# More projection work in program order ahead of the triangular solve's first product

## The chip, the cores and the metric

The kernel runs on one core of a Trainium2 chip. The time is the device time of one execution in microseconds (us), as the median of several runs. Three runs of the kernel before gave 3366.3, 3369.54 and 3373.71 us. One further execution was recorded by the hardware profiler; all durations quoted below come from it.

The engines are called as in the profile: PE (TensorE matmul), PEld (its weight loads), DVE (VectorE), ACT (ScalarE), POOL (GpSimd) and SP (SyncE, whose queue issues nearly all DMAs here).

## The reference, cut to what matters

Two models run one after the other on 512 tokens of width 1024. The change touches only the mixer of the first model, which occurs twice (two layers). In each layer it computes, in outline:

```
proj = rmsnorm(x) @ w_in                      # q,k,v of attention; q,k,v of delta net; z; two gates
y_attn = grid_attention(rope(q), rope(k), v) @ w_o_attn
...
a_kk  = strictly lower part of (k_beta @ k.T) * decay      # 64 x 64, per head, chunk and direction
t_inv = triangular_solve(eye + a_kk, eye)                  # "the solve"
...
for chunk in chunks:                                       # "the scan"
    v_new = u - w @ state;  o = q_dec @ state + qk @ v_new
    state = state * g_tot + k_dec.T @ v_new
...
mixed = sigmoid(gate0) * y_attn + sigmoid(gate1) * (norm(o) * silu(z) @ w_o_dn)
x = x + mixed @ w_out
```

## The kernel before, in words

Activations lie with features on the 128 partitions and the 512 tokens along the free dimension. A weight matrix comes in 1 MB pieces of 256 columns (`fetch`, L465; two buffers), is split into a high and a low part by an ACT cast and a POOL subtraction (`wload`, L478 and the helper `tt`, L384; four buffers each), and multiplies the split activations in three matmuls per 128 x 128 block (`proj`, L491, L494, L495). One projection of 128 output columns over 1024 inputs is 24 matmuls of 512 columns; one over 512 inputs is 12. Results land in one of two PSUM banks (`psb`) until DVE or ACT has read them.

The mixer (`_mix`) is written as several Python generators that emit instructions piece by piece. Each `yield` gives a number, an estimate of how long that piece takes. `Side` (L1065) takes such a main generator and, after each of its pieces, lets side generators emit until their own sum has caught up. So the numbers decide only where in the program text a piece of side work stands. These generators matter here:

- `solve` (L1020) loads the 64 triangular matrices into the tile N with two DMAs (from `scrT`, L1023, and from `scrN`, L1024), yields, and then does 30 steps on DVE. Each step is one product into a PSUM bank and one addition back into N (both through L384) and yields 2.1 * (2j(31-j)+66)/960, together 26.0. A memset of the diagonal (L1035) follows in program order, then five copies, and the results go out by DMA (L1050). The PSUM bank is the only one of its kind in this stage (`psg`, one buffer by `banks(2, 3, 1)`, L1096); the attention core needs the same bank for its value products (L976).
- `qkv` (L894): projection of the attention key (6), then its norm, rotation (`turn`, L887), the value projection, eight copies (L912) and the splits of key and value (6).
- `queries(g)` (L916): two query projections (6 each), then norm, rotation and eight small DMAs (2).
- `gate_logits` (L1003): eight projections of the first gate (G1 to G8 below) and eight of the second (H1 to H8), 6 each.
- `core` (L941): the attention itself, with `queries(1)` in its middle; it is given with a factor 0.6.
- `scan` (L1243): sixteen steps of the delta net's scan, with a factor 0.25; beside it `branch` (L1012) emits eight output projections of 12 matmuls (B1 to B8), 3 each. While the scan runs, each gate or branch projection is pinned behind the last matmul of the scan step emitted before it.

The program order is not yet the order of the engine queues. The whole program is laid out by the tile framework (L1800, `schedule_with_timeline_sim=True`), which fills each engine's queue by its own forecast of when operands will be ready; program order sets only the priority among instructions that it takes to be ready. Semaphore waits, once placed, hold up everything behind them in the same queue.

The part that sets the order around the change is this (L1102 to L1114):

```python
heads = chain(qkv(), queries(0))
side = Side(merge(heads, islice(gates, G2)), gates)
side.beside(solve(at), R2)
...
side.gens.append(islice(gates15, 8 - E1 - E2))
side.beside(core(), R4)
last.append(pv_last[0])
for _ in islice(gates15, E2):
    pass
```

with G2 = 2, E1 = 1, E2 = 3, R2 = 1, R4 = 0.6.

Of the kernel before, what the change touches and what calls it, by code (L numbers as in the profile page):

```python
# [305 lines left out]
class Prog:  # L306
# [341 lines left out]
    def _mix(self, l, nm, nxt, mp):  # L648
# [371 lines left out]
        def solve(sp):  # L1020
            tmp, pt = sp.tile([P, 1024], F32, name="ntmp"), self.psg()
            Nm = N[:, :4096].rearrange("p (j i) -> p j i", j=64)
            nc.sync.dma_start(out=Nm[64:128], in_=scrT.rearrange("j c p (h i) -> (c p h) j i", h=2))  # L1023
            nc.sync.dma_start(out=Nm[0:64], in_=scrN.rearrange("c p (h j) i -> (c p h) j i", h=2))  # L1024
            yield 5

            Nh = N.rearrange("p (a x) -> p a x", a=2)[:, :, :2048].rearrange("p a (j i) -> p a j i", i=64)
            for j in range(1, 31):
                n = 31 - j
                t = pt[:, :2 * j * n].rearrange("p (a c i) -> p a c i", a=2, c=j)  # L1030
                self.tt(t, Nh[:, :, 0:j, j:j + 1].broadcast_to((P, 2, j, n)),
                        Nh[:, :, j:j + 1, j + 1:32].broadcast_to((P, 2, j, n)), ALU.mult)
                self.tt(Nh[:, :, 0:j, j + 1:32], Nh[:, :, 0:j, j + 1:32], t, ALU.add)
                yield 2.1 * (2 * j * n + 66) / 960.0
            nc.vector.memset(N[:, 0:4096:65], 1.0)  # L1035


            fw, bw = Nm[0:64], Nm[64:128]
            i0, i1 = slice(0, 32), slice(32, 64)
            flip = lambda v: v.rearrange("p j i -> p i j")  # L1040
            first = tmp[64:128].rearrange("p (j i) -> p j i", j=32)
            nc.gpsimd.tensor_copy(bw[:, i1, i0], bw[:, i1, i1])
            nc.scalar.copy(fw[:, i1, i0], flip(fw[:, i0, i0]))
            nc.vector.tensor_copy(first, flip(bw[:, i0, i0]))
            nc.vector.tensor_copy(bw[:, i1, i1], flip(bw[:, i1, i0]))
            nc.scalar.copy(bw[:, i0, i0], first)
            for s_ in range(4):
                for d in range(2):
                    c = 3 * d + (1 - 2 * d) * s_
                    nc.sync.dma_start(out=scrI[d][c].rearrange("c p h j i -> (c p h) (j i)"),  # L1050
                                      in_=N[d * 64 + c * 16:d * 64 + c * 16 + 16, :4096])
            yield 5
# [49 lines left out]
# [3 lines that stand above are left out]
        for _ in heads:  # L1105
            pass
# [698 lines left out]
```

## Time and profile before

| | |
|---|---|
| three runs | 3366.3, 3369.54, 3373.71 us |
| profiled execution, whole time | 3364.51 us |
| its span, first to last instruction | 3362.7 us |
| mean granted TensorE clock | 0.986 of full speed |
| PE busy | 3198.5 us, 95% of the span |
| DVE, POOL, ACT busy | 55%, 51%, 45% |

In a row of instructions the columns are: start in us, duration in us (of all in the row), engine, line, operation, output<-inputs, shapes and count; in brackets the idle time of the engine just before and what ended it. In a row of waits: engine, tile and line that waited, what it waited for, us in total, times, longest. In a table of stretches: the stretch, its length, then for each engine busy us and number of instructions, the granted TensorE clock, the DMA engines' busy share and GB/s. The first mixer's solve, attention and scan lie between 160 and 444 us of the span, the second's between 1016 and 1301 us.

### The profile page before, as it was taken

The page shows a single profiled execution, that of the slowest core. Times are in us where ns is not written, and L with a number is a line of the kernel's source. Part 1 is how long each engine was busy: PE and PEld are TensorE (multiplying, and loading weights), DVE is VectorE, ACT ScalarE, POOL GpSimd, SP SyncE. Part 2 cuts the span into 40 slices and gives each one's busy share as a digit, 9 for nine tenths or more (in the row PEclk, how much of TensorE's full clock was granted, in tenths as well). Part 3 has the DMA queues.
Part 4 walks back from the last instruction along what each step waited for, and adds up shares of the span by engine and source line. Part 5 has one row for each costly group of instructions (what it writes and reads, how often), then busy time and mean ns, then how long its engine had stood idle before and what let it go on. Part 6 is the DMA issues. An engine that isn't in the chain of part 4 may idle for free. (4 is left out here: it accounts for less than half of the span.)

```text
span 3362.7 us, 47054 instructions
## 1 busy us (share of the span) xinstructions
PE 3198.5 (95%) x17342; PEld 2643.8 (79%) x17342; DVE 1832.8 (55%) x3549; ACT 1499.9 (45%) x2804; POOL 1719.1 (51%) x1453
## 2 busy tenths in 40 slices
PE   8988799999998889999999998999999999999999
PEld 6767678888776677788887777878888888888887
DVE  7687556463678855555366675453223676453222
ACT  5646444343564643443353335543334455544332
POOL 4542375444554236544456556565556336555554
PEclk9999999999999999999999999999999999999999
DMA  4632532222355254322222113234223223222222
GB/s 155 179 94 67 136 118 99 97 92 94 125 162 136 69 124 129 126 90 99 100 102 88 63 47 129 91 124 132 90 99 110 73 69 126 95 91 93 99 100 88
DMA packets 142013, 353.03 MB, mean 105 GB/s; under 512 B 44079, under 2 KB 81327, under 8 KB 113112
## 3 DMA queue, kind: packets, MB, share of 16 engines
q1 hardware_dynamic: 140352, 346.53, 32.0%
q10 hardware_dynamic: 1432, 3.49, 0.4%
q8 instruction: 138, 2.26, 0.3%
q14 instruction: 91, 0.75, 0.1%
HBM read 316.34 MB, written 34.16 MB: 104 GB/s over the span
## 5 line engine op out<-in xcount | busy, mean ns | idle before, releaser
L384 POOL TENSOR_TENSOR wlo<-wraw,whi 128x512 fp32r<-128x512 f32 (+2 forms) x1044 | 1353.1, 1299 | 1420.8 <-ACT whi L478 1382.6
L478 ACT CAST whi<-wraw 128x512 fp32r<-128x512 f32 (+2 forms) x1044 | 633.4, 608 | 1141.0 <-PE psb L494 863.7
L491 PE MATMUL psb<-act,whi 128*128 128x512 f32 x1888 | 750.8, 398 | 25.4 <-ACT whi L478 12.6
L495 PE MATMUL psb<-act,wlo 128*128 128x512 f32 x1888 | 746.3, 396 | 0.6 <-POOL wlo L384 0.4
L494 PE MATMUL psb<-act,whi 128*128 128x512 f32 x1888 | 746.3, 395 | 0.6 <-DVE act L277 0.6
L491 PEld LDWEIGHTS psb<-act,whi 128*128 128x128 f32 x1888 | 359.0, 190 | 101.9 <-ACT whi L478 14.1
L495 PEld LDWEIGHTS psb<-act,wlo 128*128 128x128 f32 x1888 | 358.0, 190 | 76.5 <-POOL wlo L384 3.0
L494 PEld LDWEIGHTS psb<-act,whi 128*128 128x128 f32 x1888 | 358.6, 190 | 73.7 <-DVE act L277 2.0
L384 DVE TENSOR_TENSOR x<-psb,x 128x512 f32<-128x512 f32 x168 | 115.1, 689 | 380.3 <-PE psb L495 380.0
L491 PE MATMUL ps<-act,whi 128*128 128x512 f32 (+1 forms) x720 | 282.8, 393 | 3.4 <-ACT rB L303 3.4
L494 PE MATMUL ps<-act,whi 128*128 128x512 f32 (+1 forms) x720 | 282.2, 392 | 0.0
L495 PE MATMUL ps<-act,wlo 128*128 128x512 f32 (+1 forms) x720 | 281.9, 391 | 0.0
L491 PE MATMUL psb<-mid,whi 128*128 128x512 f32 x704 | 277.1, 394 | 1.0 <-DVE x L384 1.0
L495 PE MATMUL psb<-mid,wlo 128*128 128x512 f32 x704 | 276.3, 393 | 0.0
L494 PE MATMUL psb<-mid,whi 128*128 128x512 f32 x704 | 273.9, 389 | 0.0
L491 PEld LDWEIGHTS ps<-act,whi 128*128 128x128 f32 (+1 forms) x720 | 135.0, 188 | 34.3 <-ACT rB L303 4.9
L495 PEld LDWEIGHTS ps<-act,wlo 128*128 128x128 f32 (+1 forms) x720 | 135.0, 188 | 29.7
L494 PEld LDWEIGHTS ps<-act,whi 128*128 128x128 f32 (+1 forms) x720 | 135.0, 187 | 29.3
L495 PEld LDWEIGHTS psb<-mid,wlo 128*128 128x128 f32 x704 | 132.3, 188 | 30.5
L491 PEld LDWEIGHTS psb<-mid,whi 128*128 128x128 f32 x704 | 132.7, 188 | 29.2 <-DVE x L384 1.5
L494 PEld LDWEIGHTS psb<-mid,whi 128*128 128x128 f32 x704 | 132.2, 188 | 29.2
L384 DVE TENSOR_TENSOR cv<-ps,cv 128x512 f32<-128x512 f32 (+1 forms) x60 | 41.5, 692 | 188.7 <-PE ps L495 106.8
(431 smaller groups left out, 5441.9 us busy)
## 6 DMA issues: line engine op xcount, KB each, us to landing
wraw<-in_wup SPq DMA_DIRECT2D x44, 1024.0 KB, 4.8
wraw<-in_fup SPq DMA_DIRECT2D x44, 1024.0 KB, 4.8
wraw<-in_win SPq DMA_DIRECT2D x38, 1024.0 KB, 4.8
wraw<-in_wdn SPq DMA_DIRECT2D x16, 1024.0 KB, 4.8
wraw<-in_evin SPq DMA_DIRECT2D x16, 1024.0 KB, 4.8
wraw<-in_xakv SPq DMA_DIRECT2D x16, 1024.0 KB, 4.9
wraw<-in_fdn SPq DMA_DIRECT2D x16, 1024.0 KB, 4.9
wraw<-in_odin SPq DMA_DIRECT2D x12, 1024.0 KB, 4.8
```

The lines of the kernel that those rows point to most:

```text
L384: getattr(self.nc, eng).tensor_tensor(out, a, b, op)
L478: nc.scalar.copy(hi, part)
L491: mm = nc.tensor.matmul(ps, hi[:, i], acts[k][:, 0, :n], start=k == 0, stop=False)
L494: nc.tensor.matmul(ps, hi[:, i], acts[k][:, 1, :n], start=False, stop=False)
L495: nc.tensor.matmul(ps, lo[:, i], acts[k][:, 0, :n], start=False, stop=k == kc - 1)
```

## The change

One number changes: what `solve` yields between its two loads and its first product.

```diff
@@ -1022,7 +1022,7 @@
             Nm = N[:, :4096].rearrange("p (j i) -> p j i", j=64)
             nc.sync.dma_start(out=Nm[64:128], in_=scrT.rearrange("j c p (h i) -> (c p h) j i", h=2))
             nc.sync.dma_start(out=Nm[0:64], in_=scrN.rearrange("c p (h j) i -> (c p h) j i", h=2))
-            yield 5
+            yield 18
 
             Nh = N.rearrange("p (a x) -> p a x", a=2)[:, :, :2048].rearrange("p a (j i) -> p a j i", i=64)
             for j in range(1, 31):
```

The program order that follows from the numbers, with j1 to j30 for the solve's steps, q0 and q1 for the two groups of queries (a, b: projections; c: norm and rotation) and "core" for pieces of attention:

```
before: load qkvA j1-j3 G1 j4-j10 qkvB j11-j15 G2 j16-j21 q0a j22-j28 q0b j29 j30 end q0c
        | core with G3 G4 G5 G6 q1a G7 q1b q1c G8 H1 H2 H3 | H4 H5 H6
        | scan0 H7 ... scan6 B1 ... scan9 B2 ... scan12 B3 ... scan15 B4 | B5 B6 B7 B8 H8
after:  load qkvA G1 qkvB j1 G2 j2-j9 q0a j10-j15 q0b j16-j20 q0c j21 j22 G3 j23-j30 G4 end
        | core with G5 G6 G7 G8 q1a H1 q1b q1c H2 H3 H4 | H5 H6 H7
        | scan0 B1 ... scan3 B2 ... scan6 B3 ... scan9 B4 ... scan12 B5 ... scan15 B6 | B7 B8 H8
```

No instruction is added, removed or altered.

## Rows read from the trace of the kernel before

**Rows 1.** The page of the profile: span, busy time, and the group of POOL's weight subtractions.

```profile
span 3362.7 us, 47054 instructions
PE 3198.5 (95%) x17342; PEld 2643.8 (79%) x17342; DVE 1832.8 (55%) x3549; ACT 1499.9 (45%) x2804; POOL 1719.1 (51%) x1453
...
L384 POOL TENSOR_TENSOR wlo<-wraw,whi 128x512 fp32r<-128x512 f32 (+2 forms) x1044 | 1353.1, 1299 | 1420.8 <-ACT whi L478 1382.6
```

**Rows 2.** Stretches: busy us of each engine, clock; the first mixer, one later stretch.

```profile
192.40:208.50 16.10, 16.09 (x66) 13.26 (x67) 15.29 (x25) 5.79 (x10) 11.22 (x8) 0.86 0.27 83
208.50:244.70 36.20, 34.88 (x160) 27.16 (x158) 35.79 (x77) 18.53 (x39) 13.50 (x11) 1.00 0.27 95
244.70:248.40 3.70, 0.00 (x0) 0.00 (x0) 3.67 (x10) 0.00 (x0) 1.02 (x1) 0.96 0.00 0
248.40:269.30 20.90, 17.19 (x109) 14.71 (x110) 15.39 (x26) 17.90 (x35) 1.86 (x1) 0.93 0.51 102
295.70:325.70 30.00, 25.21 (x162) 20.21 (x161) 24.46 (x50) 23.55 (x54) 1.65 (x2) 1.00 0.12 40
422.30:443.60 21.30, 21.30 (x104) 17.47 (x101) 15.18 (x32) 7.29 (x13) 9.93 (x8) 1.00 0.21 63
650.00:700.00 50.00, 50.00 (x221) 41.25 (x221) 20.22 (x23) 16.81 (x27) 23.85 (x18) 1.00 0.27 96
```

**Rows 3.** Waits of PE, 150 to 215 us, then 1016 to 1067 us (second mixer).

```profile
PE ps L416 <- ACT cv L884: 6.3, 1, 6.3
...
PE ps L416 <- ACT cv L884: 6.0, 1, 6.0
```

**Rows 4.** The DVE queue in order of time around the first product, both mixers.

```profile
183.76 0.23 DVE L384 TENSOR_TENSOR ps<-N 128x60 f32<-128x60 f32 x1 [5.41 <-DMA N<-scrT]
...
184.06 0.11 DVE L1035 MEMSET N<- 128x64 f32 x1
...
184.47 0.69 DVE L384 TENSOR_TENSOR th<-th,cv 128x512 f32<-128x512 f32 x1
...
186.57 0.34 DVE L384 TENSOR_TENSOR ps<-N 128x168 f32<-128x168 f32 x1
...
1033.37 0.69 DVE L384 TENSOR_TENSOR th<-th,cv 128x512 f32<-128x512 f32 x1 [0.66 <-POOL th L384]
1040.15 0.23 DVE L384 TENSOR_TENSOR ps<-N 128x60 f32<-128x60 f32 x1 [6.09 <-DMA N<-scrT]
```

**Rows 5.** The ACT queue: readers of the query projections q0a and q1a, q1b.

```profile
191.75 0.60 ACT L884 ACTIVATE cv<-psb 128x512 f32<-128x512 f32 x1 [0.95 <-DVE ka L502]
...
267.11 0.70 ACT L883 ACTIVATE th<-psb,vect 128x512 f32<-128x512 f32 x1
...
269.15 0.71 ACT L883 ACTIVATE th<-psb,vect 128x512 f32<-128x512 f32 x1
```

**Rows 6.** Waits of PE, 215 to 300 us, then the scan, 345 to 422 us.

```profile
PE ps L976 <- DVE N L384: 3.8, 1, 3.8
...
PE ps L1202 <- DMA kes<-dnscr: 5.6, 2, 3.1
```

**Rows 7.** DVE groups by operation, 150 to 270 us: the solve's products and additions.

```profile
L384 DVE TENSOR_TENSOR ps<-N 128x60 f32<-128x60 f32 (+14 forms) x30 | 21.6, 719 | 5.7 <-DMA N<-scrT 5.4
L384 DVE TENSOR_TENSOR N<-N,ps 128x60 f32<-128x60 f32 (+14 forms) x30 | 14.9, 495 | 0.3
```

**Rows 8.** The tail behind the scan: DVE, then POOL, in order of time.

```profile
436.20 1.33 DVE L1016 SCALAR_TENSOR_TENSOR x<-x,psb 128x512 f32<-128x512 f32 x2
437.45 2.43 DVE L1294 SCALAR_TENSOR_TENSOR of<-ps,vect,z 128x256 f32<-128x256 f32 x6
...
440.22 2.56 POOL L502 TENSOR_TENSOR ydn<-of,ydn 128x512 fp32r<-128x512 f32 x2 [1.58 <-ACT ydn L500]
```

**Rows 9.** The DVE queue: readers of the gate projections G3 and G4.

```profile
200.69 0.69 DVE L384 TENSOR_TENSOR x<-psb,rB 128x512 f32<-128x512 f32 x1 [0.53 <-PE psb L495]
...
209.50 0.68 DVE L384 TENSOR_TENSOR x<-psb,rB 128x512 f32<-128x512 f32 x1
```

## The prediction

> **What bounds the kernel now.** I read the page first: PE is busy for 95% of 3362.7 us [rows 1], so only stretches in which PE stands idle, or work that PE does anyway but at another place, can move the time. Then I split the first mixer into stretches (the second repeats them) and compared each with a later stretch that PE fills without a gap [rows 2]. That stretch also gives the price of a projection: 221 matmuls in 50.0 us are 0.226 us each, so a gate projection (24) is 5.4 us and a branch projection (12) is 2.7 us. Third, the waits of PE: near the solve's start the longest is 6.3 us, in the second mixer 6.0 us [rows 3]; in both PE waits for the square of a query projection, L884 on ACT. Fourth, the queues behind that wait. ACT's L884 had to wait until DVE was done with the split of the rotated key, because it writes into a buffer that this split reads [rows 5]. And DVE had stood still for 5.4 us (6.1 in the second mixer) at the solve's first product, which waited for the load of N [rows 4]. So the load's lateness passes through the DVE queue and the ACT queue to PE.
>
> What matters most is what the DVE queue shows about order. The memset L1035 comes last of the solve's DVE work before the copies in program order, yet it runs behind the first product [rows 4]. The rotation's last addition (th<-th,cv) belongs to qkvB, which the program emits after j10, yet in the second mixer it runs ahead of j1, and in the first only j1 and the memset's neighbours pass it [rows 4]. So program order is priority only; an instruction is queued when the layout forecasts its operands ready, and the layout forecast the load to land some 5 us before it did.
>
> **The change part by part.** No instruction is new; everything is a matter of place. The profiled execution took 3364.5 us, of which the span is 3362.7; it lies 5.0 us under the median of 3369.5. The terms below are differences and are put on the median.
>
> (a) *The head.* G1 and qkvB now precede j1. G1 and G2 were done before the load landed, and qkvB's chain up to the value projection as well, so their new priority moves nothing. At the moment when the layout took N as landed, j1 was the one ready instruction on DVE: in the first mixer even the memset followed before the rotation's last addition [rows 4]. A lower priority does not hold back an instruction that has no competitor. I therefore expect j1 in its old place and the stall of 5.4 and 6.1 us to stay. What moves are the eight copies (L912) and the key's splits, which now pass the second addition and the third step; those three instructions cost some 0.2 to 0.35 us each (the third product: 0.34 [rows 4]). L884 comes forward by so much: 0.6 us taken, ends 0 and -0.9.
>
> (b) *The attention.* From the solve to the start of the scan the program now holds 15 gate projections, not 14: +5.4 us of PE work. What can hide it: PE idles for all of 244.7 to 248.4, when the core's value product waits for the solve's last addition (same bank, 3.8 us [rows 6]), for 20.9 - 17.2 = 3.7 us of 248.4 to 269.3, and for 4.8 us of 295.7 to 325.7 [rows 2]. In the first two PE has no projection at all, because both psb banks hold q1a and q1b, whose readers on ACT run only at 267.1 and 269.2 [rows 5]. After the change G7 and G8 go ahead of q1a, and H1 stands between q1a and q1b, so in those 25 us one bank stays free for H1 and then q1b: 10.8 us of work over 7.4 us of idle time. ACT, busy for 17.9 of 20.9 us there [rows 2], must cast their weights in between. I take 4.0 us as hidden: +1.4 us. Ends: nothing hidden +5.4; all 7.4 hidden -2.0.
>
> (c) *The scan.* The pinned work inside it has the same sum, 13.5 us (H7, B1 to B3 before; B1 to B5 after), but half of the 5.4 us at its start goes to step 3. PE waits for DMA-loaded keys (kes) twice there, 5.6 us in all [rows 6], the first time 2.5 us long, close behind step 3. B2 fits into it: -2.0 us taken. Ends -2.6 (the whole wait) and +2.7 (B2 lands ahead of a chain step that waited for nothing).
>
> (d) *The tail.* Behind the last scan step PE had five branches and H8, 21.3 us without a gap [rows 2]; now three branches and H8, 5.4 us less. But the first two operands of the next product (ydn) are written by POOL until 442.8 [rows 8], less than a us before the old end of that cover at 443.6. The chain that makes them gets faster only by the two branch readers (1.33 us) ahead of its scalings on DVE [rows 8]. So the tail ends at about 441.5 and PE idles for some 3 us: -2.1 us taken. Ends -0.8 (chain unmoved) and -5.4 (the cover was the limit).
>
> (e) *The solve's end.* j10 and later lose priority to q0a, q0b and q0c, j23 and later to G3. DVE is full there (35.8 of 36.2 us [rows 2]), but G3 and G4 were already done at 200.7 and 209.5 [rows 9], before the solve's middle, so the set of instructions ahead of the solve's last addition hardly changes: 0, with the ends in (b).
>
> Sum per mixer: -0.6 + 1.4 - 2.0 - 2.1 = -3.3 us; two mixers -6.6 us: 3369.5 - 6.6 = **3362.9 us**. A measurement of this kernel tells about 0.2%, 6.7 us, from no change, so this lies on the edge between faster and the same.
>
> The solve's products read both inputs from SBUF, its additions one from PSUM, and the products took 21.6 us against 14.9 us for the same elements [rows 7]; what else reads SBUF meanwhile may be the cause of these 6.7 us (R3). The Trainium skill ("SBUF — State Buffer", section "SBUF: two separate sides") has a rule that speaks against the change here: a DVE instruction with two SBUF inputs and a GpSimd instruction exclude each other for a whole instruction. By that rule the solve would get longer with every POOL subtraction put beside it; the products' excess agrees with it.
>
> **The rivals.**
>
> *R1: the change does what its place in the program says.* The products fall behind the key's tail, DVE copies and splits while the load is under way, L884 comes some 5 us earlier, and PE's wait of 6.3 and 6.0 us shrinks to about 1. PE's clock, 0.86 in the 16.1 us behind the wait [rows 2], where some matmuls run at the lower of its two levels, would gain up to 2.3 us. Price: about -6 us per mixer on top of the sum, 3362.9 - 12 = 3351 us. For it: in the second mixer j1 follows the rotation's addition directly, so a small shift of the forecast would let all copies pass. Against it: j1 stood alone when it was queued.
>
> *R2: slower, by lost cover.* The work that (b) puts ahead of the scan hides nothing, since PE's holes there are made by waits on DVE and ACT that move along with the projections, and the tail does not shorten because its own chain ends it. The place is the stretch from 244.7 to 325.7 and ydn behind the scan; the price is +5.4 - 0.8 = +4.6 us per mixer, 3369.5 + 9.2 = 3379 us. It decides if less than about 1 us of the 5.4 is hidden. For it: ACT's load in (b), and ydn's end at 442.8 [rows 8].
>
> *R3: the solve ends later.* Two more gates beside the solve bring four more POOL subtractions of 1.3 us [rows 1]; each in front of a product they would add up to 5.2 us per mixer to the wait of 3.8 us [rows 6], and with the other terms 3369.5 + 10.4 - 6.6 = 3373 us. Against it: G3 and G4 ran beside the solve before [rows 9].
>
> *R4: nothing.* The layout is greedy, so projections go where PE was free in either case, and all terms cancel: 3369 us.
>
> **How the numbers follow.** The sum as forecast, 0.55: it stands on the edge, so 0.27 faster, 0.25 the same, 0.03 slower. R1, 0.15, all faster. R2, 0.12, slower; R3, 0.03: 0.02 the same, 0.01 slower. R4, 0.15: 0.11 the same, the rest split. Together faster 0.44, the same 0.38, slower 0.18. The range goes from below R1 (two more us per mixer for the clock, 3347) to R2 less its last 2 us (3377); the likeliest case alone has 3356 ((d) at its lower end) to 3371 ((b) with nothing hidden).
>
> **What would show it.** Right: DVE still idles for 5 to 6 us on the load of N with j1 ahead of most copies; the wait of PE for L884 falls by less than 1 us; projection matmuls appear between 245 and 269 us; a branch fills the first wait for kes; a gap of 2 to 4 us opens on PE ahead of the first ydn product. Wrong: the eight copies ahead of j1 and PE's wait near 1 us (R1); no projections between 245 and 269 us and the scan starting 4 to 5 us later (R2); the value product's wait for N above 6 us (R3).

## The result and the profile after

The change makes the kernel slower. Four runs gave 3391.37 to 3400.86 us, median 3394.78, against 3369.5 us; the ratio is 1.0084, with an interval of 1.0063 to 1.0105, about 28 us (the two medians differ by 25.3). The profiled execution has a span of 3389.6 us, 26.9 more than before. The page, its lines as in [rows 1]:

```profile
span 3389.6 us, 47035 instructions
PE 3215.7 (95%) x17342; PEld 2653.6 (78%) x17342; DVE 1836.7 (54%) x3549; ACT 1500.2 (44%) x2804; POOL 1722.2 (51%) x1453
```

The same work on every engine, so the time went into waits and a lower clock, and the PE line tells how much into each. For the same 17342 matmuls PE is busy for 3215.7 us, not 3198.5: 17.2 of the 26.9 us. The granted clock, 0.981 instead of 0.986 over the span, comes to the same by an estimate: 3389.6 x 0.019 - 3362.7 x 0.014 = 17.3 us. Only the other 9.7 us are idle time of PE.

A residual addition behind the first mixer comes 16.9 us later than before, one behind the second 26.9 us later, and that stays to the end: the loss lies in the two mixers. I cut each mixer at five events that both traces show: the value projection read by PE (L524), the core's first value product (L976), the square sums of q1 (L416), the last value product, the last output product of the scan (L1236), the first product with ydn (L491). Lengths in us, first / second mixer:

| stretch | before | after |
|---|---|---|
| 1: head and solve | 70.0 / 72.7 | 70.8 / 70.0 |
| 2: first value product to q1's sums | 20.8 / 20.9 | 31.2 / 32.9 |
| 3: to the last value product | 56.6 / 56.7 | 58.1 / 58.1 |
| 4: gates and scan | 96.5 / 96.0 | 100.8 / 96.8 |
| 5: tail | 21.2 / 21.2 | 17.5 / 17.5 |

The ten stretches hold 21 of the 26.9 us, stretch 2 alone 10.4 and 12.0; the rest lies outside these cuts. Of the first mixer, the kernel after (columns as in [rows 2]; the cuts are rounded to 0.1 us):

```profile
180.00:250.80 70.80, 64.38 (x277) 51.07 (x278) 65.60 (x128) 30.44 (x58) 29.90 (x22) 0.93 0.30 88
250.80:282.00 31.20, 22.80 (x134) 18.66 (x133) 18.28 (x30) 19.20 (x40) 5.91 (x5) 0.95 0.43 102
282.00:340.10 58.10, 48.20 (x263) 38.87 (x262) 43.41 (x85) 34.25 (x73) 13.66 (x10) 0.94 0.11 32
340.10:440.90 100.80, 82.59 (x1349) 69.08 (x1348) 53.05 (x131) 41.66 (x100) 35.54 (x61) 0.92 0.58 127
440.90:458.30 17.40, 15.77 (x76) 12.89 (x76) 14.90 (x32) 6.71 (x12) 6.63 (x5) 1.00 0.24 67
```

And the kernel before, cut at the same events:

```profile
178.40:248.40 70.00, 58.70 (x252) 46.42 (x252) 63.14 (x129) 28.40 (x56) 27.58 (x21) 0.92 0.32 91
248.40:269.30 20.90, 17.19 (x109) 14.71 (x110) 15.39 (x26) 17.90 (x35) 1.86 (x1) 0.93 0.51 102
269.30:325.90 56.60, 51.37 (x287) 41.75 (x285) 44.46 (x86) 35.67 (x75) 16.26 (x12) 1.00 0.14 47
325.90:422.40 96.50, 78.13 (x1349) 66.02 (x1348) 52.67 (x130) 42.12 (x101) 35.58 (x61) 0.98 0.56 130
```

The counts of PE matmuls tell what moved, since a gate is 24: one gate more in stretch 1 (252 to 277) and in stretch 2 (109 to 134), one less in 3 (287 to 263), and two branches of 12 less in 5. Stretch 1 took its gate in 0.8 us, and stretch 3 gave nothing back for the one that it lost: it ran at a granted clock of 0.94, not 1.00. In stretch 2 PE is busy for 5.6 us more and idle for 4.7 us more. The waits of PE, 150 to 215 us, the second mixer's head, and 250 to 284 us, which answer to [rows 3, 6]:

```profile
PE ps L416 <- ACT cv L884: 4.0, 1, 4.0
...
PE ps L416 <- ACT cv L884: 2.4, 1, 2.4
...
PE psb L491 <- DVE gt L384: 5.1, 1, 5.1
```

The wait at the head shrank from 6.3 and 6.0 us; the one for `gt` is new. DVE's queue answers to [rows 4, 9] and names its cause:

```profile
184.10 0.23 DVE L384 TENSOR_TENSOR ps<-N 128x60 f32<-128x60 f32 x1 [4.19 <-DMA N<-scrT]
184.36 0.22 DVE L384 TENSOR_TENSOR N<-N,ps 128x60 f32<-128x60 f32 x1
184.39 0.11 DVE L1035 MEMSET N<- 128x64 f32 x1
184.62 0.29 DVE L384 TENSOR_TENSOR ps<-N 128x116 f32<-128x116 f32 x1
...
185.60 3.46 DVE L912 COPY cv<-th 32x512 f32<-32x512 f32 x8
...
264.47 0.69 DVE L384 TENSOR_TENSOR gt<-psb,rB 128x512 f32<-128x512 f32 x1 [5.76 <-DMA ti<-N]
...
1052.54 3.46 DVE L912 COPY cv<-th 32x512 f32<-32x512 f32 x8
...
1060.65 0.23 DVE L384 TENSOR_TENSOR ps<-N 128x60 f32<-128x60 f32 x1 [3.92 <-DMA N<-scrT]
```

`gt<-psb,rB` reads H1's PSUM bank. Its output tile `g1` (L1107) carries the tag "N": it takes the place of the solve's own tile, which is free only when the solve's eight transfers out (L1050) have landed. SyncE's queue shows these:

```profile
251.29 9.34 SPq L1050 DMA_DIRECT2D ti<-N  x8
```

So H1's projection is done, its bank stays taken until 264.5, q1a holds the other, and q1b's projection starts only at 265.22, after PE has idled for 5.07 us. Its matmuls start 0.43 us apart up to 267.94 and 0.23 us apart from 268.35 on: behind the wait PE ran at the lower of its two clock levels. ACT reads q1a and q1b 12.7 us later than in [rows 5]:

```profile
279.84 0.70 ACT L883 ACTIVATE th<-psb,vect 128x512 f32<-128x512 f32 x1
...
281.88 0.70 ACT L883 ACTIVATE th<-psb,vect 128x512 f32<-128x512 f32 x1
```

In the scan (waits of PE, 339.9 to 458.4 us) the wait for keys fell from 5.6 us [rows 6] to 3.2, as forecast, but a step of `join` (L1180, which puts the solve's results together for the scan) now waits behind a weight subtraction on POOL:

```profile
PE ps L1173 <- ACT offd L1165: 4.2, 4, 2.1
PE ps L1180 <- POOL wlo L384: 3.2, 1, 3.2
PE ps L1202 <- DMA kes<-dnscr: 3.2, 2, 2.8
```

The two cancel: in stretch 4 PE is idle for 18.2 us, 18.4 before. That it is 4.3 us longer is PE's busy time for the same 1349 matmuls, 82.59 us at a clock of 0.92 against 78.13 at 0.98.

In the tail, where [rows 8] show POOL's ydn, PE now waits for both halves of it:

```profile
458.32 0.73 PE L491 MATMUL psb<-ydn,whi 128*128 128x512 f32 x2 [1.65 <-ACT ydn L500]
...
459.68 0.79 PE L494 MATMUL psb<-ydn,whi 128*128 128x512 f32 x1 [0.63 <-POOL ydn L502]
```

### The profile page after: what moved, and what is told of

The parts are those of the page before. It is cut to its first block, busy times and chain, and to the rows that moved or that the text cites. A ratio compares the mean times of both kernels' runs of the same rounds, so it can differ in the third digit from the quotient of the medians.

```text
span 3389.6 us, 47035 instructions
## 1 busy us (share of the span) xinstructions
PE 3215.7 (95%) x17342; PEld 2653.6 (78%) x17342; DVE 1836.7 (54%) x3549; ACT 1500.2 (44%) x2804; POOL 1722.2 (51%) x1453
## 5 line engine op out<-in xcount | busy, mean ns | idle before, releaser
L491 PE MATMUL psb<-act,whi 128*128 128x512 f32 x1888 | 752.0, 399 | 33.0 <-ACT whi L478 13.9
L491 PEld LDWEIGHTS psb<-act,whi 128*128 128x128 f32 x1888 | 359.9, 191 | 110.2 <-ACT whi L478 14.8
L491 PE MATMUL ps<-act,whi 128*128 128x512 f32 (+1 forms) x720 | 282.4, 392 | 3.4 <-ACT rB L303 3.4
L491 PE MATMUL psb<-mid,whi 128*128 128x512 f32 x704 | 276.4, 394 | 1.0 <-DVE x L384 1.0
L491 PEld LDWEIGHTS ps<-act,whi 128*128 128x128 f32 (+1 forms) x720 | 134.9, 187 | 34.5 <-ACT rB L303 4.9
L491 PEld LDWEIGHTS psb<-mid,whi 128*128 128x128 f32 x704 | 132.3, 188 | 29.7 <-DVE x L384 1.5
```

The source lines that it names most:

```text
L491: mm = nc.tensor.matmul(ps, hi[:, i], acts[k][:, 0, :n], start=k == 0, stop=False)
```

## The experiments

Times are medians; each ratio is to runs of the kernel before on the same chip in the same session (medians 3366.6 to 3368.8 us).

**E1 and E2: the two halves of the edit.** E1 lets only the heads and G1, G2 go between load and first product; E2 keeps five steps and emits G3, G4 behind the solve.

```diff
E1, on the change:
-side = Side(merge(heads, islice(gates, G2)), gates)
+side = Side(merge(heads, islice(gates, G2)))
...
 for _ in heads:
     pass
+side.gens.append(gates)
E2, on the kernel before:
+for _ in islice(gates, 2):
+    pass
 g1 = sub.tile([P, 4160], F32, name="gt1", tag="N")
```

> Only the heads (qkvB among them) and G1, G2 go between the load of N and the first product, eighteen steps of them; G3 and later stay behind the solve as before. Theory (the loss comes from H1, whose result is written into the solve's own buffer N, standing between q1a and q1b): here H1 comes behind q1b again, no wait of PE for DVE's gt (5.1 and 3.5 us with the change), q1's readers about 13 us behind q0's as before, and the head keeps the gain that the change has in the second mixer (PE's wait for L884 2.4 us, not 6.0): 3360 to 3370 us. Rival A (the new rank of the heads itself costs, by copies and splits of the key ahead of the products): the loss stays, at least half of it, 3380 us or more.

> The mirror of the run with the heads alone: five steps go ahead of the first product as before, but G3 and G4 are emitted behind the solve ahead of the core, so that H1 falls between q1a and q1b. Theory (H1's buffer): the wait of DVE for the transfers out of N and the wait of PE for gt of some 5 us are back, q1b's readers come about 12 us late, 3385 to 3400 us. Rival A (the new rank of the heads): 3365 to 3373 us.

E1: 3368.47 us, 1.0005 [0.9995, 1.0015]. E2: 3406.39 us, 1.0109 [1.0092, 1.0126], PE's wait for gt 5.9 us. The new rank of the heads by itself costs and gains nothing that can be told; the two gates carry the loss. E2 lies above its range and above the change, and its interval overlaps that of the change: whether the heads' rank takes some of the loss back in the change is not shown.

**E3, E4, E5: H1 freed in three ways.** E3 gives H1 a buffer of its own (some small early tiles go to another pool for room). E4 yields 12, which puts G8 between the queries and H1 behind them. E5 appends the second layer's gates only behind q1c.

```diff
E3, on the change:
+h1 = mp.tile([P, S], F32, name="gt1h")
-gates15 = gate_logits(15, gt1, lambda: g1[:, len(gt1) * S:len(gt1) * S + S])
+gates15 = gate_logits(15, gt1, lambda: g1[:, len(gt1) * S:len(gt1) * S + S] if gt1 else h1)
E5, on the change, in core():
 yield from queries(g)
+side.gens.append(islice(gates15, 8 - E1 - E2))
...
-side.gens.append(islice(gates15, 8 - E1 - E2))
 side.beside(core(), R4)
```

> The change as it is, but H1's result lies in a buffer of its own and not in N (some small tiles of the beginning change their pool to make room). Theory: the wait of DVE's gt for the transfers out of N goes, PE's wait for gt goes with it, q1b runs some 8 us earlier or more, and most of the loss of 25 us comes back: 3360 to 3375 us. Rival B (an extra gate ahead of the scan costs its 5.4 us per mixer without cover, and its place on ACT and DVE the rest): within 5 us of the changed kernel, 3385 to 3400 us. Between: the buffer is one part only.

> The change as it is, eighteen steps, but the gates of the second layer come into the order only after q1c is emitted, so that nothing stands between q1a and q1b but G8; nothing else changes and H1 still goes into N. Theory: DVE does not meet the transfers out of N, and the loss goes: 3360 to 3372 us. Rival B (the extra gate ahead of the scan costs by itself): still 10 us or more above the kernel before, 3380 us.

> Twelve steps instead of eighteen: one gate more than before (G3, not G3 and G4) goes beside the solve, so G8 and not H1 stands between q1a and q1b; H1 comes behind q1c, seven gates of the second layer still ahead of the scan, branches from its first step on. Theory (two parts: H1 between the queries costs some 12 us, the fifteenth gate ahead of the scan with what follows from it in the scan some 8 to 10): as the run with H1 late, 3377 to 3385 us, no wait for gt. Rival (what is left in that run comes from two gates beside the solve, which make its end later): half of it, 3370 to 3376 us.

E3: 3389.03 us, 1.0060 [1.0047, 1.0073]. E5: 3382.35 us, 1.0042 [1.0030, 1.0055]. E4: 3385.16 us, 1.0055 [1.0042, 1.0068]. PE's wait for H1's reader in N was gone in all three, and half of the loss or more was still there: my theory of the buffer alone fell. In E3 stretches 1 to 3 are still 7.9 and 6.9 us longer than before in the two mixers. All three still had a fifteenth gate ahead of the scan, so that became the second suspect.

**E6, E7, E8: each part alone.** E6 is E5 with H7 back at the scan's first step, where it was before. E7 is the kernel before with H7 ahead of the scan. E8 is the kernel before with H1 in G7's place, between q1a and q1b.

```diff
E6, on E5:
-for _ in islice(gates15, E2):
+for _ in islice(gates15, E2 - 1):
...
+side.gens.append(islice(gates15, 1))
 side.gens.append(branch(self.A["woa"][l], yT, gt0))
E7, on the kernel before:
-side.gens.append(islice(gates15, 8 - E1 - E2))
+side.gens.append(islice(gates15, 7 - E1 - E2))
-for _ in islice(gates15, E2):
+for _ in islice(gates15, E2 + 1):
E8, on the kernel before:
-side = Side(merge(heads, islice(gates, G2)), gates)
+side = Side(merge(heads, islice(gates, G2)), islice(gates, 4))
-side.gens.append(islice(gates15, 8 - E1 - E2))
+side.gens += [islice(gates15, 2), gates, islice(gates15, 6 - E1 - E2)]
```

> Eighteen steps, H1 and later only behind q1c, and H7 moved out of the stretch ahead of the scan to its first step, as before, with three branches in the scan and four behind it: what is left of the change is the order of the head and the two gates beside the solve. Theory: back to the kernel before within 0.2%, 3365 to 3375 us, the tail 21 us again, the scan 96 us. Rival (the solve's end and the core's start cost): as the run with H1 late alone, 3378 us or more.

> The kernel before (five steps), but H7 goes ahead of the scan and the branches start at its first step: the second part of the theory alone. Per mixer 5.4 us of projection with no idle time of PE to go into, up to 4 us more in the scan, 3.7 us back in the tail: 2 to 6 us per mixer, 3373 to 3381 us. Rival (the fifteenth gate is free, the loss lies in the head): 3366 to 3371 us.

> The kernel before, but H1 and G7 change places, so that H1 stands between q1a and q1b (H2 follows behind q1c, then G7 and G8); fourteen gates ahead of the scan, the rest as before: the first part of the theory alone. Expected: DVE waits for the transfers out of N, PE for gt some 5 us, q1's readers 8 to 12 us later, 3378 to 3392 us. Rival (H1 costs only together with the other parts): below 3374 us.

E6: 3368.29 us, 1.0009 [1.0000, 1.0018]: no loss left. E7: 3374.83 us, 1.0025 [1.0013, 1.0036], +8.3 us. E8: 3384.70 us, 1.0056 [1.0043, 1.0068], +18.1 us. Either part costs by itself. E7's stretches 4 and 5:

```profile
326.80:432.20 105.40, 87.29 (x1373) 73.93 (x1371) 53.83 (x132) 43.55 (x103) 38.12 (x63) 0.94 0.56 124
432.20:449.70 17.50, 15.86 (x78) 12.98 (x77) 14.96 (x33) 6.76 (x12) 6.64 (x6) 1.00 0.22 68
```

The gate (1349 to 1373 matmuls) made stretch 4 longer by 8.9 us, more than its own 5.4, and the tail gave back 3.7. That is the first mixer; there PE's idle time in stretch 4 did not grow (18.1 us, 18.4 before), and what goes beyond the 5.4 us is the clock, 0.94 instead of 0.98.

**E9 and E13: place or buffer.** E9 is E8 with E3's buffer, E13 the kernel before with that buffer and nothing else.

> The run with H1 in G7's place alone, but H1's result in a buffer of its own. If H1's 18 us are the wait for the transfers out of N (DVE stood 5 us, in two mixers), at least half of them go: 3369 to 3377 us. If they are the place itself (a projection between q1a and q1b that PE has to do where nothing covers it, in a bank that q1b needs), they stay: 3380 to 3387 us.

> The kernel before with nothing but the buffer of its own for H1 and the small tiles moved for it; the order is that of before, H1 behind q1b. If the gain of 3.8 us of the run with H1 early in its own buffer is H1's place: here within 0.1% of the kernel before, 3364 to 3370 us. If it is the moved tiles or the buffer: 3360 to 3364 us.

E9: 3362.90 us, 0.9986 [0.9976, 0.9996], below both of its ranges. E13: 3365.97 us, 0.9997 [0.9987, 1.0006]. Between E8 and E9 lies the buffer alone, some 22 us. Who reads H1's bank, and when, in E8:

```profile
263.39 0.69 DVE L384 TENSOR_TENSOR gt<-psb,rB 128x512 f32<-128x512 f32 x1 [3.08 <-DMA ti<-N]
```

and in E9:

```profile
236.03 0.68 DVE L384 TENSOR_TENSOR gt1h<-psb,rB 128x512 f32<-128x512 f32 x1
```

With its own buffer H1 is read at 236.0, while the solve still runs, as G7 was before (236.27); in N it is read 27 us later. The idle 3.08 us in brackets is the smaller part of the cost: the layout had already put H1 late. Stretches 1 and 2 of E8, then of E9, show what that moved:

```profile
178.30:248.20 69.90, 52.91 (x229) 40.96 (x229) 61.36 (x129) 27.00 (x54) 25.40 (x19) 0.90 0.35 94
248.20:280.60 32.40, 25.85 (x132) 21.64 (x133) 16.27 (x27) 19.71 (x38) 4.46 (x3) 0.84 0.32 66
...
176.90:248.20 71.30, 59.40 (x253) 46.87 (x253) 63.02 (x130) 28.45 (x57) 27.80 (x21) 0.91 0.34 92
248.20:269.30 21.10, 18.25 (x109) 15.89 (x110) 15.40 (x26) 17.94 (x35) 1.87 (x1) 0.86 0.50 100
```

In E8 a whole projection has gone from stretch 1 (229 matmuls, 253 in E9), which is 1.4 us shorter without it, to stretch 2 (132, 109 in E9), where PE is busy for 7.6 us more and idle for 3.7 us more. The intervals of E9 and E13 overlap, so a gain of the place by itself is not shown.

**E14 and E15: buffer and gate, two by two.** Both are the change with E6's move of H7 (fourteen gates); E14 has the buffer of its own as well.

> The change with H1 in a buffer of its own and H7 moved from ahead of the scan to its first step: of the three parts only H1's place between q1a and q1b is left. If the parts add in this order of the program: the fifteenth gate is worth 8 to 12 us, so 3377 to 3381 us, some 10 us above before for H1's place alone (its 5.4 us of PE behind the solve's end, with nothing to cover them). If the place costs nothing once the buffer is free: 3364 to 3371 us.

> The change with nothing undone but H7, which goes to the scan's first step as before; H1 stays between q1a and q1b and in N. If the parts add: 25 to 28 less 8 to 12 us, 3380 to 3388 us. If the fifteenth gate is the condition for H1's cost: below 3375 us.

| eighteen steps | own buffer | in N |
|---|---|---|
| fourteen gates | E14 3369.99, 1.0008 [1.0000, 1.0017] | E15 3390.48, 1.0065 [1.0053, 1.0078] |
| fifteen gates | E3 3389.03, 1.0060 [1.0047, 1.0073] | the change 3394.78, 1.0084 [1.0063, 1.0105] |

With neither fault the change costs nothing that can be told; either brings about 20 us; both bring 28. E15 lies above its range, and the interval of the change overlaps those of E3 and E15, so that two faults cost more than one is not shown. The buffer is worth 0.24% (the change to E3), 0.57% (E15 to E14) and 0.70% (E8 to E9), the gate 0.19% (the change to E15), 0.25% (E7 to before), 0.33% (E5 to E6) and 0.52% (E3 to E14): both are there, and neither has one price. Stretches 2 and 4 of E14:

```profile
250.20:276.30 26.10, 21.00 (x134) 17.66 (x133) 18.16 (x30) 19.24 (x40) 5.95 (x5) 1.00 0.52 121
...
334.10:423.80 89.70, 73.62 (x1325) 62.95 (x1323) 51.87 (x129) 40.35 (x98) 32.97 (x59) 0.94 0.57 137
```

of E15:

```profile
251.70:283.40 31.70, 24.54 (x134) 20.15 (x134) 18.49 (x30) 19.33 (x40) 6.02 (x5) 0.89 0.43 100
...
341.90:437.00 95.10, 78.30 (x1326) 67.31 (x1324) 52.04 (x129) 40.45 (x98) 32.97 (x59) 0.89 0.57 129
```

and of E3:

```profile
250.00:276.10 26.10, 20.95 (x134) 17.61 (x133) 18.14 (x30) 19.26 (x40) 5.96 (x5) 1.00 0.52 121
...
333.90:436.60 102.70, 83.72 (x1350) 70.87 (x1348) 53.25 (x131) 41.68 (x100) 35.59 (x61) 0.92 0.55 125
```

Stretch 2 is clean: 26.1 us with the buffer, whatever the number of gates, and 31.2 or 31.7 without: 5.1 to 5.6 us for N (second mixer: 24.4 and 26.1 with the buffer, 31.2 and 32.9 without, 6.8 us). Stretch 4 is not: 89.7, 95.1, 102.7 and 100.8 us, at a granted clock of 0.94, 0.89, 0.92 and 0.92. The fourteen gates differ by 5.4 us in it, the fifteen by 1.9 the other way, and there the sums stop adding up. PE's busy time tells why. For the same matmuls, 1325 and 1326, PE is busy for 73.62 us in E14 and 78.30 in E15, and idle for 16.1 and 16.8: 4.7 of the 5.4 us are a slower clock. In the second mixer it is the other way round, 90.6 us in E14 and 88.9 in E15 at 0.94 and 0.96, so this part is no steady price of N. What lowers the clock during the scan stays open.

**E10, E11, E12, E16, E17: rival R1 by force.** A copy of one column from the key's last split into the first product's bank must run before that product, and so holds it behind all copies and splits (E10, on E1). E11 also moves the two copies behind the solve (L1044, L1045) to POOL; E12 does both on E6. E16 (on E1) and E17 (on E14) hold the memset too, by a second column in N.

```diff
E16 and E17; E10, E11 and E12 have the copy into pt alone:
 yield 18
+for t in (pt, N):
+    nc.vector.tensor_copy(t[:, 0:1], att["k"][1][:, 1, 0:1].bitcast(F32))
```

> The heads alone go ahead of the first product (fourteen gates ahead of the scan, H1 behind q1b), and a copy of one column from the key's last split into the product's PSUM bank holds the first product behind all copies and splits of the key: rival R1 of the prediction by force. If the wait at the head is worth its length: PE's wait for L884 near 1 us in both mixers, 3356 to 3363 us. If the solve's end sets the core anyway: the solve ends 1 to 3 us later for the copies in front of it, the head's gain turns into waiting for N, 3364 to 3371 us.

> As the run with the head tied, and the two DVE copies behind the solve's last addition (1.0 and 1.1 us, ahead of the core's splits in DVE's queue) go to POOL, which was busy for 1.9 of the 20.9 us there. If these copies hold up the core: 1 to 2 us less per mixer than the run with the head tied alone; if PE's other waits cover them, the same within 3 us.

> The run with eighteen steps, H1 late and fourteen gates ahead of the scan, with the first product held behind the key's splits and the two copies behind the solve on POOL. There PE waited 3.6 us for a split (pTl) behind those copies, and the stretch from the first value product to q1's readers took 2.6 and 3.7 us longer than before. If the copies are the cause: 3358 to 3364 us; if not: 3366 to 3372 us.

> The heads alone ahead of the first product, and two copies of one column from the key's last split, one into the product's PSUM bank and one into N, so that first product and memset both stand behind all copies and splits of the key in DVE's queue. If the wait at the head is worth its length (R1): q0's square sums some 5 us earlier, PE's wait for L884 near 1 us in both mixers, 3354 to 3363 us. If the solve's end sets the core: its last addition comes at the same time or 1 to 2 us later, PE's gain at the head turns into waits for N or for the splits of the core, 3364 to 3374 us.

> The change with H1 in a buffer of its own, fourteen gates ahead of the scan and the same two tied columns. If the head's wait is worth its length here: 3356 to 3364 us. If the solve's end sets the core: 3366 to 3374 us, as without the ties.

E10: 3378.59 us, 1.0029 [1.0019, 1.0039], outside both expectations. E11: 3378.68 us, the same ratio: POOL's copies are worth nothing there. E12: 3364.31 us, 0.9991 [0.9982, 0.9999], lies between its two ranges and decides nothing. In E10's queue DVE still stood for 4.76 us, and the memset of N (L1036 there) and the rotation's last addition start together behind that. I read it as the memset waiting for the load ahead of the addition; the row names no wait ("issue"), but in E16, where the memset is tied too, the addition starts after 0.66 us:

```profile
183.41 0.66 DVE L384 TENSOR_TENSOR th<-th,cv 128x512 f32<-128x512 f32 x1 [4.76 <-issue]
183.44 0.11 DVE L1036 MEMSET N<- 128x64 f32 x1
```

So E10 delayed the solve without freeing the head, and tests nothing of R1. Of the 10 us that it loses against E1, 1.4 and 1.3 lie in stretch 1 of the two mixers and 4.7 and 2.6 in stretch 4; why there is open. E16: 3368.70 us, 1.0000 [0.9991, 1.0009]. E17: 3359.10 us, 0.9972 [0.9960, 0.9983], 9 us faster than before and the fastest version here. Waits of PE in E16, 150 to 252 us:

```profile
PE ps L967 <- DVE pTl L384: 5.5, 3, 3.2
...
PE ps L976 <- DVE N L384: 3.2, 1, 3.2
...
PE ps L416 <- ACT cv L884: 0.8, 1, 0.8
```

The head's wait fell from 6.3 to 0.8 us, and PE waited for the core's splits and the solve instead. Stretch 1 of E16:

```profile
178.50:246.50 68.00, 56.85 (x253) 44.80 (x253) 63.84 (x132) 28.14 (x57) 28.01 (x21) 0.97 0.30 91
```

and stretches 1 and 2 of E17:

```profile
178.20:245.10 66.90, 61.10 (x276) 47.87 (x276) 64.98 (x132) 29.05 (x58) 30.15 (x22) 1.00 0.37 99
245.10:269.10 24.00, 21.03 (x132) 17.69 (x133) 16.29 (x28) 20.03 (x39) 6.00 (x4) 1.00 0.52 132
```

E17 has a gate more in stretch 1 (276 matmuls to 253) and is 1.1 us shorter there; its stretch 2, 24.0 us, holds H1 as E14's 26.1 us do. In E17 the clock of stretch 1 is 1.00, against 0.93 in E14, and of the 6.4 us between them (73.3 to 66.9) 3.4 are busy time of PE for the same 276 matmuls and 3.0 idle time. So the time won at the head was kept with another gate ready for PE, and lost again in E16. That the gate is the reason is my reading: E17 differs from E16 in H1's place and buffer as well.

## Why the prediction was wrong

I forecast 3362.9 us and a range to 3377; the result lies 18 us beyond it, on the side that I gave 0.18.

- **(a) The head: right in the first mixer.** j1 stayed in its place, DVE stood 4.2 us, all eight copies passed the third step, L884 came 1.0 us sooner (190.79 instead of 191.75), and E1 puts the whole part within the noise. PE's wait fell by 2.3 us, more than I had said, because PE also came to it 1.3 us later. In the second mixer all copies passed j1, which I gave to R1; PE's wait fell to 2.4 us and stretch 1 by 2.7, and stretch 2 took more than that back.
- **(b) The attention: here the prediction failed**, in the sentence "one bank stays free for H1 and then q1b". I counted PSUM banks and idle time of PE, and did not ask where H1's result goes. It goes into N, so its reader waits for the solve's transfers out and the bank stays taken. Stretch 2 took 10.4 and 12.0 us more, where I had +1.4 for the whole part. The bank is about half of that: with H1 in its own buffer (E3) 5.1 and 6.8 us of it go. The other half, 5.3 and 5.2 us, is a second step that failed: 4.0 of 5.4 us hidden. The hiding in stretch 1 was right: PE did 5.7 us more there (58.70 to 64.38 busy) for 0.8 us, and no longer waited for N. But two gates had to be hidden ahead, not one, because one came out of stretch 3, which is set by its own chain: 56.6 us with 287 matmuls before, 57.8 to 58.5 with 263 (E14, the change, E15). There a gate was free, and taking it out gained nothing; the 4.8 idle us of 295.7 to 325.7 [rows 2] that I named as room lie in this stretch.
- **(c) The scan: the mechanism was right, the sum wrong.** The wait for keys shrank by 2.4 us, but the branches' weights put 3.2 us of POOL's queue ahead of `join`, so that PE's idle time stayed. The +4.3 and +0.8 us instead of -2.0 are no price of this part: in the eight profiles with before's order there (before, E1, E8, E9, E10, E11, E13, E16) stretch 4 takes 93.2 to 100.9 us, at clocks of 0.93 to 1.00.
- **(d) The tail: right.** It is 3.7 us shorter instead of 2.1; ACT and POOL finish ydn 1.65 and 0.63 us after PE asks for it. Behind the cut 2.1 us are lost again in the first mixer and 0.7 in the second (the product with ydn starts 14.75 and 26.2 us later than before, the residual addition 16.9 and 26.9), so that -1.6 and -3.0 us are left.
- **(e) The solve's end: right.** E6 has the two extra gates beside the solve and stays within 1.0018. The solve's products took 21.6 us in both traces, so R3's subtractions did not lengthen it.
- **The clock: put at nothing.** My sum prices a matmul at 0.226 us, the full clock of [rows 2], and has no term for the clock; only R1 and the range speak of it. PE's longer time for the same matmuls is 17.2 of the 26.9 us of the profile. Part of it follows the waits below, as behind the 5.07 us for `gt`; in stretch 4 the cause is open.
- **The rivals.** R2 had the right sign and, for the gate alone, nearly the right price: 9.2 us forecast, 8.3 in E7, though as +8.9 and +8.0 in stretch 4 and -3.7 in the tail of each mixer, not as +5.4 and -0.8. Its reason, a gate that nothing hides, is also what stretch 2 of E3 shows. R1's price of 6 us per mixer shows only in E17 against E14 (11 us in all), where H1 has its own buffer; E16 has the same short wait at the head and no gain. R4 is out.

## What to carry to other kernels

When a projection is moved ahead, follow its result as well as its operands: the tile that its reader writes may be another stage's buffer, and then a PSUM bank is held until that stage's transfers have landed. Work beside a stretch that is bound by its own chain was free here and cost its full length elsewhere, so count instructions per stretch before and after, not idle time alone. Compare PE's busy time for the same matmuls too: two thirds of this loss were a lower clock, which a count of waits does not show. A wait taken away at the head paid only in the version that had more work ready to run in it; try the two together, not only one at a time.

## What the runs showed of the hardware

The solve's products, two inputs from SBUF, stretched under POOL's subtractions while its additions, with one input from PSUM, did not. In E17, DVE's queue:

```profile
185.42 0.81 DVE L384 TENSOR_TENSOR ps<-N 128x60 f32<-128x60 f32 x1
186.28 0.21 DVE L384 TENSOR_TENSOR N<-N,ps 128x60 f32<-128x60 f32 x1
...
186.52 1.02 DVE L384 TENSOR_TENSOR ps<-N 128x116 f32<-128x116 f32 x1
187.58 0.28 DVE L384 TENSOR_TENSOR N<-N,ps 128x116 f32<-128x116 f32 x1
187.89 0.34 DVE L384 TENSOR_TENSOR ps<-N 128x168 f32<-128x168 f32 x1
```

and POOL's:

```profile
184.34 3.06 POOL L384 TENSOR_TENSOR wlo<-wraw,whi 128x512 fp32r<-128x512 f32 x2 [5.54 <-ACT whi L478]
```

The third product, behind POOL's end at 187.40, took 0.34 us, as in [rows 4]. The first two took 0.23 and 0.29 us in the kernel after, where POOL's next subtraction comes at 190.30:

```profile
190.30 3.26 POOL L384 TENSOR_TENSOR wlo<-wraw,whi 128x512 fp32r<-128x512 f32 x2 [9.77 <-ACT whi L478]
```

This agrees with the Trainium skill ("SBUF — State Buffer", section "SBUF: two separate sides"), by which a DVE instruction with two SBUF inputs and a GpSimd instruction that reads SBUF exclude each other. I had weighed the rule as a danger of several us per mixer; thirty products together took 22.6 us in E17 and 21.6 before.
